# Last attention head: where the eight blocks of the output projection stand among its score blocks

## The chip, the cores and the metric

The kernel runs on one core of a Trainium2 chip. The metric is the device time of one execution in microseconds (us), as the median of several runs. PE is the matrix engine (PEld its weight loads), DVE the vector engine, ACT the scalar engine, POOL the general one; SP issues most of the DMA transfers.

## The reference

A decoder trunk of two layers on 1024 tokens with 1024 features, in float32. The first layer mixes with a short gated convolution, the second with multi-head attention over a shared compressed key and value; each is followed by a gated feed-forward part. The change lies at the end of the attention:

```python
def causal_block_attention(...):          # per head h, query block of 128
    sc = qn_b . k_nope + qr_b . k_pe      # 128 + 64 features
    p = softmax(where(mask, sc * scale, neg))
    return p @ v
...
h = h + attn.reshape(b, s, N_HEADS * V_HEAD_DIM) @ w_o
h = h + swiglu_ffn(rms_norm(h, mla_ffn_norm_g[j]), ...)
```

There are 8 heads of 128 value features. `h` is the residual stream, and the product with `w_o` sums over all heads.

## The kernel before

**Number format.** Every float32 product is made of three matmuls on a high and a low part of each operand (`split`, L108 to L112: ACT casts the high part, DVE or POOL subtracts for the low part). The residual stream lies transposed: `st.h[n]` holds features 128 n to 128 n + 127 for all 1024 tokens.

**A head.** `scores` (L1459) makes one block of 128 queries against the keys up to it: five terms of matmuls into PSUM, then mask, maximum and scaling on DVE, the exponential on ACT (L1476, the last reader of the PSUM tile), the division on DVE. Blocks 0 to 3 fit one bank (`ps1`), blocks 4 to 7 take a wide buffer of two banks (`ps2`). `pv` (L1481) makes the value product of four query blocks at once: transposes on PE (L1491), casts and subtractions into `pt`, three matmuls per key block (L1500 to L1502). A head has two value products: g = 0 (blocks 0 to 3) and g = 1 (blocks 4 to 7). The second one of a head is kept in `pend` and issued within the next head, ahead of its score blocks 4 and 5 (L1590).

**The loop of the heads** (L1574). Four times per head it issues a pair of score blocks, and behind the pair the jobs that `per` (L1586) names. In heads 0 to 6 the jobs prepare the next head. In head 7 they are eight blocks of the output projection, `project_o(O0, 0, (n,))` for n = 0 to 7: block n makes features 128 n to 128 n + 127 of the attention's output from heads 0 to 4, whose values were written to DRAM and read back (`O0`, L1600). Each block loads its weights into a raw buffer (320 KB), splits them (high part on ACT, low part on POOL, L112), loads `st.h[n]` from DRAM on the SP queue (L1549), runs 30 matmuls of 512 columns (L146 to L150) into a wide PSUM buffer, and adds the result to `st.h[n]` on DVE (L1552).

**Behind the loop** (L1601 to L1605). The weights of heads 5, 6 and 7 are loaded (`wo_load`, raw buffers), those of head 5 split (`wo_parts(5)`, two slots), and the second value product of head 7 issued. Then the stage `pl` adds heads 5 to 7 to `st.h` and leads into the feed-forward part; the splits for heads 6 and 7 are its first steps.

**What is scarce.** "act" slots: 30 tiles of 512 KB, for `h`, keys, values, queries, read-back heads and kept weights. Raw buffers: 5, two of which hold read-back parts (`cq_tile`). High and low weight tiles: 4 each; both parts of a block's weights take low ones (`wsplit`), so two blocks have theirs at a time, and `pt` takes the high ones. PSUM in the attention: two wide buffers and four single banks; `pl` has eight single banks of a new pool.

**What sets the order.** The loop of the heads isn't written as a fixed order: the framework's planner orders each engine's queue before the run, by its own estimate of when operands and buffers are ready, with the order of the text as priority. On the chip every queue then runs in that fixed order. The stages before and after (`Steps.run`) are in an order written out by hand, which the planner keeps.

Of the kernel before, what the change touches and what calls it, by code (L numbers as in the profile page):

```python
# [19 lines left out]
KD = D // P  # L20
# [28 lines left out]
def trunk(ctx, tc, aps, out):  # L49
# [7 lines left out]
    def enter(name):  # L57

        if "stack" in phase:
            phase["stack"].close()  # L60
        phase["stack"] = ExitStack()
        phase["pool"] = phase["stack"].enter_context(tc.tile_pool(name=name, bufs=1, reuse_waits="tile"))
# [21 lines left out]
    def hi_tile(name):  # L84
        return slots.tile([P, S], F32R, name=name, tag="whi", bufs=4)
# [4 lines left out]
    def pslot(name, tag, bufs, dt=F32, shape=None):  # L90
        return phase["pool"].tile(shape or [P, S], dt, name=name, tag=tag, bufs=bufs)
# [10 lines left out]
    def ps1(name):  # L102
        return phase["psum"].tile([P, 512], F32, name=name, tag="ps1", bufs=phase["ps"][1])

    def move(dst, src):
        nc.gpsimd.dma_start(dst, src)


    def split(hi, lo, src, gain=None, eng=None):
        if gain is None:  # L110
            nc.scalar.copy(out=hi, in_=src)  # L111
            (eng or nc.vector).tensor_tensor(lo, src, hi.bitcast(F32), ALU.subtract)  # L112
        else:
            nc.scalar.activation(hi, src, AF.Copy, scale=gain)
            nc.vector.scalar_tensor_tensor(lo, src, gain, hi.bitcast(F32), ALU.mult, ALU.subtract)
# [1170 lines left out]
    def cq_tile(i):  # L1286
        return slots.tile([P, S], F32R, name="cq", tag="raw", bufs=5)
# [122 lines left out]
    def make_k(h, w=None, new=lambda: ps2("ps_k")):  # L1410
        wh, wl = w or W_k(h).all()
        ps = new()
        gemm(ps, lambda k: wh[:, k, :], lambda k: wl[:, k, :], kv_p(0), kv_p(1), range(2))
        Kt[h] = parts_of("k", ps)

    def make_v(h, w=None, quarters=None):

        wh, wl = w or W_v(h).all()
        if h not in Vt:
            Vt[h] = Vt[h + 1] = [(slot("vh", F32R), slot("vl", F32R)) for _ in range(2)]  # L1420
        nt = 4 if quarters is None else 2
        for t4 in range(2) if quarters is None else quarters:
            ps = ps2("ps_v") if nt == 4 else ps1("ps_v")
            for tb in range(nt):
                tok = slice((t4 * nt + tb) * P, (t4 * nt + tb + 1) * P)
                o = ps[:, tb * 256:(tb + 1) * 256]
                for k in range(2):
                    xh, xl = kvs[k].p
                    nc.tensor.matmul(o, lhsT=xh[:, tok], rhs=wh[:, k, :], start=k == 0, stop=False)
                    nc.tensor.matmul(o, lhsT=xh[:, tok], rhs=wl[:, k, :], start=False, stop=False)  # L1430
                    nc.tensor.matmul(o, lhsT=xl[:, tok], rhs=wh[:, k, :], start=False, stop=k == 1)
            c = slice(t4 * nt % 4 * 256, (t4 * nt % 4 + nt) * 256)
            split(*[t[:, c] for t in Vt[h][t4 * nt // 4]], ps)

    def make_q(h, w=None, new=lambda: ps2("ps_q")):
        wh, wl = w or W_q(h).all()
        ps = new()
        gemm(ps, lambda k: wh[:, k, :], lambda k: wl[:, k, :], q_p(0), q_p(1), range(3))
        a, b = parts_of("qn", ps)
        Qt.setdefault(h, {}).update(h=a, l=b)  # L1440

    def make_qr(h, w=None, new=lambda: ps2("ps_q"), eng=nc.gpsimd):

        hi, lo = w or W_qr(h).all()
        ps = new()
        gemm(ps, lambda k: hi[:, k, :], lambda k: lo[:, k, :], q_p(0), q_p(1), range(3))
        qr = tmp("qr")
        rope(qr, ps, eng)
        yh, yl = tmp("qrh", dt=F32R), tmp("qrl", dt=F32R)
        split(yh, yl, qr, eng=eng)  # L1450
        for a in range(2):
            t = slot("qrs", F32R)
            for i, y in enumerate((yh, yl)):
                for q in range(2):
                    r = i * 64 + q * 32
                    move(t[r:r + 32], y[q * 64 + a * 32:q * 64 + a * 32 + 32])
            Qt.setdefault(h + a, {})["r"] = t
# [23 lines left out]
    def pv(V, g, ps_, h):  # L1481

        nb = 4 * g + 4
        o = ps1("ps_pv")
        PT = {}

        def turn(kb):
            c = slice(max(kb - 4 * g, 0) * P, 512)
            t = ps1("ps_t")
            for j in range(c.start // P, 4):  # L1490
                nc.tensor.transpose(t[:, j * P:(j + 1) * P], ps_[j][:, kb * P:(kb + 1) * P], ident)  # L1491
            pt = hi_tile("pt")
            PT[kb] = pt[:, :512], pt[:, 512:]
            split(PT[kb][0][:, c], PT[kb][1][:, c], t[:, c])

        def product(kb):
            c = slice(max(kb - 4 * g, 0) * P, 512)
            vh, vl = [t[:, kb % 4 * 256 + h % 2 * P:kb % 4 * 256 + h % 2 * P + P] for t in V[kb // 4]]
            th, tl = [t[:, c] for t in PT[kb]]
            nc.tensor.matmul(o[:, c], lhsT=vh, rhs=th, start=kb == 0, stop=False)  # L1500
            nc.tensor.matmul(o[:, c], lhsT=vh, rhs=tl, start=False, stop=False)
            nc.tensor.matmul(o[:, c], lhsT=vl, rhs=th, start=False, stop=kb == nb - 1)  # L1502

        for kb in range(nb + 2):
            if kb < nb:
                turn(kb)
            if kb >= 2:
                product(kb - 2)
        gs = slice(g * 512, (g + 1) * 512)
        if h in Od:  # L1510
            split(Od[h][0][:, gs], Od[h][1][:, gs], o)
            return
        oh, ol = (pslot("oh", "oh", 1, F32R, [P, 512]), pslot("ol", "ol", 1, F32R, [P, 512]))
        split(oh, ol, o)
        move(od[h, 0, :, gs], oh)
        move(od[h, 1, :, gs], ol)
# [19 lines left out]
    def load_o(k, hi, lo):  # L1536
        move(hi, od[k, 0])
        move(lo, od[k, 1])
        return hi, lo

    def project_o(O, k0, ns, t=None, final=None):

        nk = len(O)
        hi, lo = wsplit("wo", w_o[:, k0:k0 + nk, ns[0] * P:(ns[-1] + 1) * P], [P, nk, len(ns) * P])
        for i, n in enumerate(ns):
            c = slice(i * P, (i + 1) * P)
            if t is None:
                st.h[n] = slot("h")
                nc.sync.dma_start(st.h[n], hd[n])  # L1549
                ps = ps2("ps_wo")  # L1550
                gemm(ps, lambda k: hi[:, k, c], lambda k: lo[:, k, c], lambda k: O[k][0], lambda k: O[k][1], range(nk))
                nc.vector.tensor_tensor(st.h[n], ps, st.h[n], ALU.add)  # L1552
                continue
            ts = slice(t * 512, (t + 1) * 512)
            ps = ps1("ps_wo")
            for k in range(nk):
                three(ps, hi[:, k, c], lo[:, k, c], O[k][0][:, ts], O[k][1][:, ts], k == 0, k == nk - 1)
            nc.vector.tensor_tensor(st.h[n][:, ts], ps, st.h[n][:, ts], ALU.add)
            final(n, t)
# [14 lines left out]
    for h in range(H):  # L1574
        if h >= 6:
            Od[h] = (tmp("oth", dt=F32R), tmp("otl", dt=F32R))
        if h + 1 < H:
            jobs = [lambda h=h: make_k(h + 1), lambda h=h: make_q(h + 1)]
            if h % 2:
                jobs = [lambda: make_qr(h + 1), lambda: make_v(h + 1)] + jobs  # L1580
        else:
            O1 = [load_o(5, r_(), r_())] + [Od[6], Od[7]]
            jobs = [lambda n=n: project_o(O0, 0, (n,)) for n in range(KD)]
        if h == 0:
            jobs = [lambda: make_q(1)]
        per = {1: ((0,), (), (), ()), 2: ((), (0,), (1,), ()), 4: ((0,), (1,), (2,), (3,)), 8: ((0, 1), (2, 3), (4, 5), (6, 7))}[len(jobs)]  # L1586
        p = []
        for i in range(4):
            if i == 2 and pend:
                pv(*pend.pop(0))  # L1590
            p += [scores(Kt[h], Qt[h], 2 * i + d) for d in range(2)]
            if i == 2:
                pv(Vt[h], 0, p[:4], h)
            if i == 3:
                pend.append((Vt[h], 1, p[4:], h))
            for j in per[i]:
                jobs[j]()
        if h == 6:
            r_ = lambda: slot("oth", F32R)
            O0 = [load_o(k, r_(), r_() if k < 3 else cq_tile(4 - k)) for k in range(5)]  # L1600
# [2 lines left out]
    wo_parts(5)  # L1603
    for u in pend:
        pv(*u)  # L1605
    enter("ffn")
    enter_psum(0, 8)

# [127 lines left out]
```

## Time and profile before

| | us |
|---|---|
| median of 3 runs | 2098.05 |
| lowest and highest | 2097.63, 2100.79 |
| the profiled execution | 2095.82 |
| its span in the profile | 2093.7 |

| engine | busy us | share of the span |
|---|---|---|
| PE | 2053.9 | 98% |
| PEld | 1704.7 | 81% |
| DVE | 1463.5 | 70% |
| ACT | 855.7 | 41% |
| POOL | 269.4 | 13% |

The profile is one execution, recorded by the hardware. A row of the timeline is a run of equal instructions: start, length, engine, line, output and inputs, and in brackets the idle time before it and what ended it. Starts count from the begin of the span. A matmul's end is modelled, so starts are the safer measure.

### The profile page before, as it was taken

What the parts mean: (1) busy time and instruction counts of PE and PEld (TensorE: products, weight loads), DVE (VectorE), ACT (ScalarE), POOL (GpSimd) and SP (SyncE); (2) the same over time, 40 slices, a digit from 0 to 9 for tenths busy, and PEclk for the clock granted to TensorE, in tenths of its full rate; (3) what the DMA queues carried; (4) which work ended last, traced back from release to release, by engine and by line L of the source; (5) the groups of instructions that cost most, each with busy time, mean ns of one, the idle gap of its engine ahead of it and who ended that gap; (6) DMA issues with size and microseconds to landing.
All of it is one profiled execution on the core that took longest, in us unless ns stands there. A gap on an engine that the chain in (4) does not pass through costs nothing.

```text
span 2093.7 us, 25560 instructions
## 1 busy us (share of the span) xinstructions
PE 2053.9 (98%) x9542; PEld 1704.7 (81%) x9542; DVE 1463.5 (70%) x2200; ACT 855.7 (41%) x1440; POOL 269.4 (13%) x388
## 2 busy tenths in 40 slices
PE   7999999999999999999999999989999999999998
PEld 6888888888888887787888888867888888888887
DVE  5996666787667668867577777437887666667556
ACT  7533433533333333354245455225433333333455
POOL 1111100121122110000023322101111111100000
PEclk9999999999999999999999999999999999999999
DMA  7355765596766586554232213425487565686553
GB/s 234 81 133 139 238 239 175 112 220 180 190 163 153 141 287 246 206 206 150 72 70 70 66 52 111 163 81 163 125 201 186 154 160 163 151 286 225 186 169 129
DMA packets 274316, 338.97 MB, mean 162 GB/s; under 512 B 18047, under 2 KB 177984, under 8 KB 273872
## 3 DMA queue, kind: packets, MB, share of 16 engines
q1 hardware_dynamic: 240144, 262.71, 38.8%
q0 software_dynamic: 33888, 74.56, 16.6%
q8 instruction: 74, 1.21, 0.2%
q14 instruction: 50, 0.41, 0.1%
q10 hardware_dynamic: 160, 0.07, 0.0%
HBM read 260.22 MB, written 126.35 MB: 185 GB/s over the span
## 4 chain that ended last, share of the span: by engine, by line
PE 88%; DVE 6%; ACT 2%; issue 2%; DMA 1%; DVEq 0%; SPq 0%; ACTq 0%
PE q L154 17%; PE q L155 17%; PE q L153 17%; PE dn L155 5%; PE dn L153 5%; PE dn L154 5%; PE ps_s L1469 4%; PE pl L153 2%; PE pl L155 2%; PE pl L154 2%; DVE wp_lo L112 1%; PE ps_t L1491 1%; PE ps_l L155 1%; PE ps_l L153 1%; PE ps_l L154 1%
## 5 line engine op out<-in xcount | busy, mean ns | idle before, releaser
L153 PE MATMUL q<-xh,w_hi 128*128 128x512 f32 x1568 | 612.4, 391 | 1.1 <-ACT xh L316 1.1
L154 PE MATMUL q<-xl,w_hi 128*128 128x512 f32 x1568 | 610.5, 389 | 2.3 <-DVE xl L317 2.1
L155 PE MATMUL q<-xh,w_lo 128*128 128x512 f32 x1568 | 610.4, 389 | 0.0
L154 PEld LDWEIGHTS q<-xl,w_hi 128*128 128x128 f32 x1568 | 294.4, 188 | 64.6 <-DVE xl L317 2.8
L153 PEld LDWEIGHTS q<-xh,w_hi 128*128 128x128 f32 x1568 | 294.3, 188 | 63.3 <-ACT xh L316 1.5
L155 PEld LDWEIGHTS q<-xh,w_lo 128*128 128x128 f32 x1568 | 294.3, 188 | 61.0
L112 DVE TENSOR_TENSOR w_lo<-wr,w_hi 128x512 fp32r<-128x512 f32 (+1 forms) x272 | 191.9, 705 | 199.3 <-ACT w_hi L111 197.5
L111 ACT CAST w_hi<-wr 128x512 fp32r<-128x512 f32 (+1 forms) x272 | 170.4, 630 | 293.5 <-DVE wr L390 191.2
L155 PE MATMUL dn<-mp_hi,wp_lo 128*128 128x512 f32 (+1 forms) x628 | 243.9, 388 | 2.6 <-DVE wp_lo L112 0.8
L153 PE MATMUL dn<-mp_hi,wp_hi 128*128 128x512 f32 (+1 forms) x628 | 242.9, 387 | 0.0
L154 PE MATMUL dn<-mp_lo,wp_hi 128*128 128x512 f32 (+1 forms) x628 | 242.0, 385 | 0.0
L1072 POOL COPY paced<-pace 128x1 f32<-128x1 f32 x128 | 75.1, 587 | 1020.4 <-ACT pace L1071 1020.4
L112 DVE TENSOR_TENSOR mp_lo<-m,mp_hi 128x1024 fp32r<-128x1024 f32 x84 | 95.2, 1134 | 120.4 <-ACT mp_hi L111 120.4
L111 ACT CAST mp_hi<-m 128x1024 fp32r<-128x1024 f32 x84 | 82.4, 980 | 221.7 <-PE dn L154 211.5
L155 PEld LDWEIGHTS dn<-mp_hi,wp_lo 128*128 128x128 f32 x628 | 117.9, 188 | 32.7 <-DVE wp_lo L112 9.6
L154 PEld LDWEIGHTS dn<-mp_lo,wp_hi 128*128 128x128 f32 x628 | 118.0, 188 | 23.6
L153 PEld LDWEIGHTS dn<-mp_hi,wp_hi 128*128 128x128 f32 x628 | 118.0, 188 | 23.0 <-DVE h L740 0.2
L112 DVE TENSOR_TENSOR wp_lo<-w,wp_hi 128x1024 fp32r<-128x1024 f32 x84 | 94.8, 1128 | 0.0
L111 ACT CAST wp_hi<-w 128x1024 fp32r<-128x1024 f32 x84 | 82.1, 977 | 0.0
L473 ACT ACTIVATE c<-c 128x512 f32<-128x512 f32 x44 | 27.8, 632 | 131.7 <-DVE c L448 131.7
L1476 ACT ACTIVATE p<-ps_s,mx,rq 128x128 f32<-128x128 f32 (+3 forms) x64 | 53.2, 833 | 55.3 <-DVE mx L1473 50.1
L382 DVE TENSOR_TENSOR w_lo<-wr,w_hi 128x1024 fp32r<-128x1024 f32 x56 | 68.2, 1218 | 7.9 <-ACT w_hi L378 7.9
(296 smaller groups left out, 3231.9 us busy)
## 6 DMA issues: line engine op xcount, KB each, us to landing
m<-md_f SPq DMA_DIRECT2D x70, 512.0 KB, 4.9
md_f<-c SPq DMA_DIRECT2D x110, 256.0 KB, 3.7
wr<-in_conv_ffn_w_dram SPq DMA_DIRECT2D x47, 512.0 KB, 6.3
wr<-in_mla_ffn_w_dram SPq DMA_DIRECT2D x47, 512.0 KB, 5.4
w<-mw_f SPq DMA_DIRECT2D x40, 512.0 KB, 3.9
h<-hd SPq DMA_DIRECT2D x32, 512.0 KB, 9.6
wr<-in_conv_w_in_dram SPq DMA_DIRECT2D x31, 512.0 KB, 5.7
mw_f<-in_conv_ffn_w_dram POOLq DMA_DIRECT2D x30, 512.0 KB, 7.7
```

Of the source, the lines that this page charges most:

```text
L111: nc.scalar.copy(out=hi, in_=src)
L112: (eng or nc.vector).tensor_tensor(lo, src, hi.bitcast(F32), ALU.subtract)
L153: nc.tensor.matmul(ps, lhsT=wh, rhs=xh, start=st, stop=False, **more)
L154: nc.tensor.matmul(ps, lhsT=wh, rhs=xl, start=False, stop=False, **more)
L155: nc.tensor.matmul(ps, lhsT=wl, rhs=xh, start=False, stop=en, **more)
L382: nc.vector.tensor_tensor(lo, self.ra, hi.bitcast(F32), ALU.subtract)
L473: nc.scalar.activation(self.C1[:, 512:], self.C1[:, 512:], self.first)
L1072: nc.gpsimd.tensor_copy(b, a)
L1469: nc.tensor.matmul(ps[:, a:b], lhsT=q[:, qs], rhs=k[:, a:b], start=i == 0, stop=i == 4)
L1476: nc.scalar.activation(p[:, :kw], ps[:, :kw], AF.Exp, bias=mx, scale=rq[:, qb:qb + 1], accum_out=rsum)
L1491: nc.tensor.transpose(t[:, j * P:(j + 1) * P], ps_[j][:, kb * P:(kb + 1) * P], ident)
```

## The change

In head 7 one block of the projection stands behind each pair of score blocks instead of two (blocks 0 to 3), and blocks 4 to 7 stand behind the second value product of head 7, after the kept weights have been loaded and head 5's split. Nothing else is altered.

```diff
-        per = {1: ((0,), (), (), ()), 2: ((), (0,), (1,), ()), 4: ((0,), (1,), (2,), (3,)), 8: ((0, 1), (2, 3), (4, 5), (6, 7))}[len(jobs)]
+        per = {1: ((0,), (), (), ()), 2: ((), (0,), (1,), ()), 4: ((0,), (1,), (2,), (3,)), 8: ((0,), (1,), (2,), (3,))}[len(jobs)]
...
     wo_parts(5)
     for u in pend:
         pv(*u)
+    for j in range(4, KD):
+        jobs[j]()
     enter("ffn")
```

In the text the order of head 7 was: score blocks 0, 1, projection 0, 1, scores 2, 3, projection 2, 3, second value product of head 6, scores 4, 5, first value product of head 7, projection 4, 5, scores 6, 7, projection 6, 7, kept weights, second value product of head 7. It becomes: scores 0, 1, projection 0, scores 2, 3, projection 1, second value product of head 6, scores 4, 5, first value product of head 7, projection 2, scores 6, 7, projection 3, kept weights, second value product of head 7, projection 4 to 7.

## Rows read from the trace of the kernel before

**Rows 1.** The page's first block: span, busy time and share of each engine.

```profile
span 2093.7 us, 25560 instructions
PE 2053.9 (98%) x9542; PEld 1704.7 (81%) x9542; DVE 1463.5 (70%) x2200; ACT 855.7 (41%) x1440; POOL 269.4 (13%) x388
```

**Rows 2.** Waits of PE, 1300 to 1412 us: total us, times, longest.

```profile
PE ps_wo L146 <- DVE h L1552: 3.6, 1, 3.6
PE ps_s L1469 <- ACT p L1476: 3.4, 2, 2.6
```

**Rows 3.** Timeline of PE, 1356 to 1406 us.

```profile
1356.67 0.68 PE L146 MATMUL ps_wo<-oth,wo_hi 128*128 128x512 f32 x2
...
1363.67 0.71 PE L146 MATMUL ps_wo<-oth,wo_hi 128*128 128x512 f32 x2
...
1370.61 0.56 PE L1469 MATMUL ps_s<-kh,qnh 128*128 128x512 f32 x2
...
1372.63 0.60 PE L1491 MATMUL ps_t<-ident,p 128*128 128x128 f32 x4
1375.84 0.73 PE L1469 MATMUL ps_s<-kh,qnh 128*128 128x512 f32 x2 [2.61 <-ACT p L1476]
...
1378.24 0.49 PE L1491 MATMUL ps_t<-ident,p 128*128 128x128 f32 x3
1382.32 1.22 PE L146 MATMUL ps_wo<-oth,wo_hi 128*128 128x512 f32 x2 [3.59 <-DVE h L1552]
...
1385.05 0.70 PE L146 MATMUL ps_wo<-oth,wo_hi 128*128 128x512 f32 x2
...
1397.42 0.49 PE L1491 MATMUL ps_t<-ident,p 128*128 128x128 f32 x3
1398.36 0.50 PE L1500 MATMUL ps_pv<-pt,vh 128*128 128x512 f32 x1 [0.46 <-ACT pt L111]
1399.49 0.50 PE L1501 MATMUL ps_pv<-pt,vh 128*128 128x512 f32 x1 [0.63 <-DVE pt L112]
...
1405.54 0.45 PE L153 MATMUL pl<-oth,wo_h 128*128 128x512 f32 x1
```

**Rows 4.** Timeline of DVE, 1379 to 1399 us.

```profile
1379.92 1.22 DVE L112 TENSOR_TENSOR wo_l<-wo_r,wo_h 128x1024 fp32r<-128x1024 f32 x1
1381.05 1.22 DVE L1552 TENSOR_TENSOR h<-ps_wo,h 128x1024 f32<-128x1024 f32 x1
...
1397.62 1.22 DVE L1552 TENSOR_TENSOR h<-ps_wo,h 128x1024 f32<-128x1024 f32 x1 [3.59 <-PE ps_wo L150]
```

**Rows 5.** Timeline of ACT, the exponential of score block 6.

```profile
1374.60 1.10 ACT L1476 ACTIVATE p<-ps_s,mx,rq 128x896 f32<-128x896 f32 x1 [3.47 <-DVE mx L1473]
```

**Rows 6.** Timeline of the SP queue: the loads of the residual tiles.

```profile
1303.43 6.38 SPq L1549 DMA_DIRECT2D h<-hd  x4
...
1354.21 0.34 SPq L1549 DMA_DIRECT2D h<-hd  x1
...
1377.07 1.55 SPq L1549 DMA_DIRECT2D h<-hd  x3
```

**Rows 7.** Windows of 20 us: busy time of each engine, granted clock, DMA share.

```profile
1380.00:1400.00 20.00, 16.59 (x66) 13.19 (x67) 9.27 (x12) 3.91 (x6) 0.00 (x0) 0.91 0.40 129
```

**Rows 8.** The blocks' raw weights: durations min/median/max, landing; waits of the SP queue.

```profile
L111 ACT CAST wo_hi<-wo_raw x8: 727/729/730, 1283.0 to 1370.4; 128x640 fp32r<-128x640 f32 x8
L112 POOL TENSOR_TENSOR wo_lo<-wo_raw,wo_hi x8: 1562/1566/1571, 1283.8 to 1371.2; 128x640 fp32r<-128x640 f32 x8
DMA to landing us min/median/max: 3.0/3.0/3.8
SPq L127 <- POOL wo_lo L112: 42.9, 5, 26.2
```

**Rows 9.** Chain of work: score block 5; timeline of PE: eight transposes of head 7.

```profile
1354.78 1.77 PE ps_s L1469 x10
...
1336.91 1.06 PE L1491 MATMUL ps_t<-ident,p 128*128 128x128 f32 x8
```

## The prediction

> **What bounds the kernel now.** I read the page's first block first: the matrix engine PE is busy for 98% of the span [rows 1], so the time is the sum of PE's work and of the few places where PE stands. Next come PE's waits over the last head, 1300 to 1412 us. The reader is to see that two waits carry most of it: 3.6 us for an addition into the residual stream (`h`, L1552) and 3.4 us in two waits for an exponential (L1476), 2.6 us of it in one [rows 2]. The PE timeline then shows where they lie [rows 3]. Output block 4 begins at 1356.67, block 5 at 1363.67, score block 6 at 1370.61. After four transposes PE waits 2.61 us, score block 7 starts at 1375.84, and after three more transposes PE waits 3.59 us, until block 6 of the projection starts at 1382.32. The last value product (queries 512 to 1023 of head 7) runs from 1397.42 to 1405.54 with waits of 0.46 and 0.63 us inside, and the first matmul of the next stage, `pl`, begins at 1405.54.
>
> Both long waits come from one knot. The attention PSUM pool has two wide buffers, shared by score blocks 4 to 7 and by all output blocks. When score block 7 is due, score block 6 holds one of them and output block 5 the other. Block 6's buffer comes free with its exponential [rows 5], and PE goes on at 1375.84. Block 5's product was done by 1370.61, but its addition runs only at 1381.05 [rows 4], because its `h` tile was not there: of the eight loads of `h`, four were issued by 1309.81, one at 1354.21, and three only from 1377.07 on, after the first matmuls of score block 7 [rows 6]. That is a count of slots. Of 30 "act" slots, 25 are held until the last scores: ten by the read-back heads 0 to 5 (two of their twelve tiles lie in raw buffers), four by `Od`, four by the values, two by the last keys, three by the last queries and two by the rotary keys. Five are left, so `h` 5 to 7 wait for score block 7, which waits for the buffer that block 5, waiting for `h`, holds, or else for block 6's softmax. The only way out is the slow one.
>
> **The change, part by part.** No instruction is added or removed. On PE 30 matmuls per block are moved for blocks 1 to 7, and with each its weight load and its load of `h` (SP queue), the cast of the weights (ACT), their low part (POOL) and the addition (DVE). The order written here is a priority: the planner takes what is ready, lower numbers first.
>
> Blocks 0 and 1 stay before score blocks 4 and 5; blocks 2 and 3, which stood there too, now come behind them. Before score block 7 only blocks 0, 1 and 2 are due, with three `h` tiles, and block 3 behind it takes the fourth; four are loaded by 1309.81 [rows 6]. Block 2's addition then frees its buffer for score block 7 at once, so the 2.61 us wait goes. No output block with a missing `h` stands in the way any more, so the 3.59 us wait goes. Score block 7's end frees seven slots; with the fifth of before that is eight: four for `h` 4 to 7, four for the kept weights of heads 5 and 6. So nothing behind it waits for a slot except head 7's kept weights, which get theirs when the values are done.
>
> After the two waits six matmuls of block 6 take 2.73 us (1382.32 to 1385.05) [rows 3]. A block's 30 take 6.94 us (1363.67 to 1370.61), that is 0.231 each, so six should take 1.39: the loss is 1.34 us. The granted clock of 1380 to 1400 is 0.91 [rows 7]: PE had worked some 3.5 us of the 9.7 before 1382.32, and the matmuls that follow run at the lower level, 1.2 instead of 2.4 GHz. With the waits gone I expect that loss to go too. The Trainium skill ("TensorE: Matmul & The Clock Gate", Part 1) speaks against counting on it: the monitor that sets the clock runs free of the kernel, so the moment of a fall differs between runs. By that, the loss may be missing from the timed runs of before; nothing in one profile decides it, and rival 4 takes it up.
>
> Removed so far: 2.61 + 3.59 + 1.34 = 7.54 us. The waits inside the last value product, 0.46 + 0.63 = 1.09 us, come from the chain transpose, cast, subtract, with an addition of block 7 (1397.62) ahead of it on DVE [rows 4]. In the changed kernel block 4 stands behind it as filler, if its weights are there in time. I take half, 0.55, between 0 and 1.09. Total 8.09.
>
> Three new waits have to be priced; before shows none of them, only their parts.
> - Block 2 takes the buffer of score block 4. The longest softmax chain shown is that of score block 6, 3.21 us from PE's last scores (1372.63) to the release (1375.84). Over it lie score block 5 (1.77 us) and eight transposes (1.06) [rows 9], and value products. 3.21 - 1.77 - 1.06 = 0.4; between 0 and 1.4 if the transposes run earlier. I take 0.3, near the covered end, since the chain of the narrower block 4 is shorter than 3.21.
> - Block 3 takes the buffer of score block 6: 3.21, covered by score block 7 (1375.84 to 1378.24, 2.40) and by transposes like the three at 1378.24 (0.49): 0.3, between 0 and 0.8.
> - `pl` now follows block 7 instead of a value product. If its first banks are those of block 7, it waits for the addition: block 7's product ended at about 1397.42 and its addition at 1398.84, so 1.42 us [rows 3, 4]; if they are others, 0. Before, `pl` followed PE's last product without a wait; I take 0.5.
>
> New waits: 1.1 us. Net: 8.1 - 1.1 = 7.0 us.
>
> The weights of blocks 4 to 7 are costed at nothing, and the cover must be named. The loads of the three kept heads now stand before theirs and hold the three raw buffers left beside the two that carry read-back heads. Block 4's weights can be loaded only when a kept head has been split, which needs score block 7's slots. I put score block 7's end near 1355, the split's end at 1358; load, cast and low part take 3.0 + 0.73 + 1.57 = 5.3 us [rows 8], so they are ready near 1364. Over that lie block 3 (6.9 us) and the value product (8.1), until about 1369. If that cover is gone, each us that the split is later than some 1363 costs one. The next block's weights need 5.3 us, under a block's 6.9. On DVE the two kept low parts (1.2 us each) may again stand before score block 7's scaling, as the one at 1379.92 did, but block 3 hides it.
>
> The profiled execution took 2095.82 us (span 2093.7 and 2.1 around it); less 7.0 it is 2088.8. It lies 2.23 under the median of the runs shown, 2098.05, and with that the forecast is 2091.0.
>
> **The rivals.** (1) The stop comes back beside the softmax: the planner gives score block 7 the buffer of score block 6 again, for instance because DVE makes block 2's addition late. For it: the planner's order already let a kept low part go ahead of a due addition [rows 4]. Against it: block 2's `h` is there and DVE is free by then. Then 2.61 stays, and the gain is 4.4 us (2093.6), or 3.1 if the clock also falls as before (2095.0).
>
> (2) It does not do what it says: the planner pulls the blocks to where they were, since it only takes the text as a priority. For it: in the trace blocks 0 and 1 run long after their place, between transposes of head 6. Against it: two wide buffers force the order of score and output blocks. Gain 0: 2098.
>
> (3) Slower: blocks 4 to 7 are starved of weights, because one raw buffer carries all four and each load waits until the block before has released it. Place: ahead of each of the four blocks; price 5.3 us each, in full 21 us, less the 7.0: 2112. It turns the gain into a loss from 1.8 us per block. For it: the SP queue waited 42.9 us in five waits for a raw buffer before [rows 8]. Against it: the split of a block waits only for the product two blocks back, whose weight tiles it takes, so one raw buffer is refilled in 5.3 us within a product of 6.9, and before, blocks 6 and 7 ran without a gap from 1385.05 to 1397.42.
>
> (4) The clock's fall belongs to this one execution: the timed runs of before don't hold the 1.34 us, so it can't be gained. For it: it is a single fall, seen in one profile. Against it: it comes right behind the longest standstill of the stage. Gain 7.0 - 1.3 = 5.7 us: 2092.4.
>
> **How the numbers follow.** Two results of this kernel are taken as different from 0.2% on, 4.2 us. The forecast has a chance of 0.55, with its own range from 8.6 us of gain (all new waits zero, the 1.09 gained) to 4.3 (2089.4 to 2093.8); rival 4 has 0.10 and lies in that range. Rival 1 has 0.19, rival 2 has 0.06, rival 3 has 0.10. Faster by over 0.2% is below 2093.85: the forecast, rival 4 and a little of rival 1, 0.67. Within 0.2%: the rest of rival 1, rival 2 and the weak end of rival 3, 0.25. Slower 0.08. For the range I take 2087.5 (those 8.6, and 1.9 for the median, whose three runs spread over 3.2 us) to 2098.5, which takes in rivals 1 and 2.
>
> **What would show it.** Right: score block 7 starts without a wait of 2 us after score block 6; no granted clock under 1.00 between the scores and `pl`; seven or eight `h` loads before the last value product; blocks 4 to 7 back to back behind it; `pl` near 1398.5. Wrong: a wait of PE for a low part of `wo` (rival 3), for an exponential before score block 7 (rival 1), or a `pl` that starts later than 1402.

## The result and the profile after

| | before | after |
|---|---|---|
| median of 4 runs each, us | 2097.88 | 2087.89 |
| lowest and highest | 2097.63, 2100.79 | 2087.49, 2090.56 |
| the profiled execution | 2095.82 | 2087.49 |
| its span | 2093.7 | 2085.4 |

The ratio is 0.9945, 95% interval 0.9933 to 0.9957: between 9.0 and 14.1 us faster. The sign and the mechanism were forecast, the size was not: 7.0 us against 10 by the medians and 11.5 by the ratio. The median of the changed kernel, 2087.89, lies just inside the low end of the range, 2087.5; by the ratio, taken of the 2098.05 that the prediction started from, it is 2086.5, just outside.

The page's first block of the changed kernel answers to [rows 1]. PE is busy 1.9 us less than before, most of it matmuls that no longer run at the lower clock; the rest of the 8.3 us of span is waiting.

```profile
span 2085.4 us, 25560 instructions
PE 2052.0 (98%) x9542; PEld 1704.3 (82%) x9542; DVE 1464.1 (70%) x2200; ACT 855.1 (41%) x1440; POOL 270.9 (13%) x388
```

The waits of PE from 1300 to 1412 us in the changed kernel (total, times, longest) answer to [rows 2]. The 3.6 us for an addition into `h` are gone. Of the two waits for an exponential, 3.4 us, the long one ahead of score block 7 is gone; the other, 0.8 us, lies ahead of head 7 and is still there. A new one of 1.4 us stands ahead of an output block.

```profile
PE ps_wo L146 <- ACT p L1476: 1.4, 1, 1.4
PE ps_s L1469 <- ACT p L1476: 0.8, 1, 0.8
PE ps_pv L1501 <- DVE pt L112: 0.6, 1, 0.6
PE ps_wo L146 <- DMA oth<-od: 0.2, 1, 0.2
```

The timeline of PE answers to [rows 3]. Score block 6 starts at 1349.59, and score block 7 at 1352.19 right behind six transposes: no stop. Block 3 stands 1.42 us at 1356.14. Block 4 follows at 1363.64, and the first matmul of `pl` at 1397.31 without a wait. The value product of head 7 lies among blocks 4 and 5.

```profile
1349.59 0.56 PE L1469 MATMUL ps_s<-kh,qnh 128*128 128x512 f32 x2
...
1351.62 0.82 PE L1491 MATMUL ps_t<-ident,p 128*128 128x128 f32 x6
1352.19 0.71 PE L1469 MATMUL ps_s<-kh,qnh 128*128 128x512 f32 x2
...
1356.14 0.73 PE L146 MATMUL ps_wo<-oth,wo_hi 128*128 128x512 f32 x2 [1.42 <-ACT p L1476]
...
1363.64 0.71 PE L146 MATMUL ps_wo<-oth,wo_hi 128*128 128x512 f32 x2
...
1370.22 0.48 PE L1500 MATMUL ps_pv<-pt,vh 128*128 128x512 f32 x1
...
1397.31 0.39 PE L153 MATMUL pl<-oth,wo_h 128*128 128x512 f32 x1
```

The SP queue's loads, against [rows 6]: two `h` loads beside the read-back of the heads instead of four, then five and one, all eight by 1355.32. The weights of block 4 (`wo_raw`) follow at 1354.82.

```profile
1304.79 0.82 SPq L1549 DMA_DIRECT2D h<-hd  x2
...
1337.29 17.44 SPq L1549 DMA_DIRECT2D h<-hd  x5
1354.82 0.38 SPq L127 DMA_DIRECT2D wo_raw<-in_mla_w_o_dram  x1
1355.32 0.47 SPq L1549 DMA_DIRECT2D h<-hd  x1
```

The 20 us window that answers to [rows 7] (length, busy time of PE, PEld, DVE, ACT, POOL, then the granted clock, DMA share, GB/s) has clock 1.00.

```profile
1380.00:1400.00 20.00, 20.00 (x92) 16.64 (x91) 4.37 (x4) 1.32 (x2) 1.58 (x1) 1.00 0.18 52
```

**The sum by starts.** A matmul's end is modelled, so I add up, from the first score matmul of head 7 to the first of `pl`, by how much each start comes later than the columns issued before it need (0.227 us for 512, the usual distance of two starts here at granted clock 1.00). Both kernels issue the same 423 matmuls there: from first to last start 95.79 us before, 86.23 after, 9.57 us less by the unrounded starts. The rows below add up to 11.94 and 2.41; in each kernel another 5.1 us is lost in small steps, most of it behind transposes, and cancels.

| us lost in this stretch | before | after |
|---|---|---|
| ahead of score block 7 | 2.83 | 0 |
| ahead of block 6 | 3.80 | 0 |
| matmuls at 1.2 GHz | 1.37 | 0 |
| inside head 7's last value product | 1.58 | 0 |
| near 1313 to 1318 (start of head 7) | 2.36 | 0.83 |
| ahead of block 3 | 0 | 1.58 |

Behind `pl` the two profiles run alike (688.2 and 688.1 us to the end). Ahead of head 7 the code is the same, but over the 13 profiled executions of this study its first matmul starts anywhere from 1308.8 to 1312.1; that scatter took 1.3 of the 9.6 back in the pair of profiles.

### The profile page after: what moved, and what is told of

The parts are those of the page before. It is cut to its first block, busy times and chain, and to the rows that moved or that the text cites. A ratio compares the mean times of both kernels' runs of the same rounds, so it can differ in the third digit from the quotient of the medians.

```text
span 2085.4 us, 25560 instructions
## 1 busy us (share of the span) xinstructions
PE 2052.0 (98%) x9542; PEld 1704.3 (82%) x9542; DVE 1464.1 (70%) x2200; ACT 855.1 (41%) x1440; POOL 270.9 (13%) x388
```

## The experiments

In all of them "the stage" is that stretch. Kernels of one group shared the runs of the kernel before: its medians there were 2099.23 us (e1 to e4) and 2099.78 (e5 to e8), 15 runs each.

**e1: only the knot undone.** The kernel before, with block 5 moved behind score blocks 6 and 7.

```diff
-        per = {... 8: ((0, 1), (2, 3), (4, 5), (6, 7))}[len(jobs)]
+        per = {... 8: ((0, 1), (2, 3), (4,), (5, 6, 7))}[len(jobs)]
```

> The order of before, with one block moved: block 5 from behind score blocks 4 and 5 to behind score blocks 6 and 7. No block stands behind the last value product. Theory (the knot of slots and wide buffers): with five blocks due before score block 7 the five h tiles suffice, so both long waits (2.8 and 3.8 us counted in starts) and the clock's loss (1.4) go, and one new wait of 1.6 us ahead of block 5 comes: -6.4 us against before, about 2091.5. Rival (filler: the gain comes from the blocks that stand behind the last value product): nothing gained, 2098 give or take 1.

2090.79 us, ratio 0.9960 (0.9948 to 0.9973), stage 88.27. One block out of the way takes both long waits and the clock's fall together. Timeline of PE of this kernel: score block 7 straight behind score block 6's transposes, block 5 with 0.29; the waits in the value product stay, since nothing is left to fill it.

```profile
1366.95 0.60 PE L1491 MATMUL ps_t<-ident,p 128*128 128x128 f32 x4
1367.31 0.70 PE L1469 MATMUL ps_s<-kh,qnh 128*128 128x512 f32 x2
...
1370.16 0.74 PE L146 MATMUL ps_wo<-oth,wo_hi 128*128 128x512 f32 x2 [0.29 <-ACT p L1476]
...
1392.03 0.50 PE L1500 MATMUL ps_pv<-pt,vh 128*128 128x512 f32 x1 [0.46 <-ACT pt L111]
1393.16 0.50 PE L1501 MATMUL ps_pv<-pt,vh 128*128 128x512 f32 x1 [0.63 <-DVE pt L112]
```

**e2: only the last two blocks moved behind the value product.**

```diff
-        per = {... 8: ((0, 1), (2, 3), (4, 5), (6, 7))}[len(jobs)]
+        per = {... 8: ((0, 1), (2, 3), (4, 5), ())}[len(jobs)]
...
     for u in pend:
         pv(*u)
+    for j in range(6, KD):
+        jobs[j]()
```

> The order of before, with blocks 6 and 7 behind the last value product and blocks 4 and 5 left where they were. Theory (the knot): block 5 is still due before score block 7 without its h tile, so score block 7 still waits 2.8 us and block 6 still waits for block 5's addition (3.8) with the clock falling; only the waits inside the value product (1.6) are filled: -1.6 us, about 2096.3. Rival (filler): two of the four blocks do half the work of the change or more: -5 us, about 2093.

2103.65 us, ratio 1.0017 (1.0007 to 1.0026), stage 100.30: slower, and neither theory had that. PE now waits 6.34 us for block 6's weights. Their load leaves only at 1381.56, because the kept heads, now ahead of it in the text, hold the raw buffers until score block 7 has freed the slots for their split (casts at 1379.12 and 1381.68), and it lands only at 1387.8, where the cast has waited for it. That is rival 3's shortage of weights, in one place instead of four. Of this kernel, one after the other, the timelines of PE, of the SP queue and of ACT:

```profile
1377.01 1.22 PE L1469 MATMUL ps_s<-kh,qnh 128*128 128x512 f32 x2 [2.61 <-ACT p L1476]
...
1388.62 1.22 PE L146 MATMUL ps_wo<-oth,wo_hi 128*128 128x512 f32 x2 [6.34 <-ACT wo_hi L111]
```

```profile
1381.56 4.92 SPq L127 DMA_DIRECT2D wo_raw<-in_mla_w_o_dram  x2
```

```profile
1387.85 0.72 ACT L111 CAST wo_hi<-wo_raw 128x640 fp32r<-128x640 f32 x1 [0.32 <-DMA wo_raw<-in_mla_w_o_dram]
```

**e3: the changed kernel with four `h` loads at the start of head 7**, as before.

```diff
-                st.h[n] = slot("h")
-                nc.sync.dma_start(st.h[n], hd[n])
+                for m in range(4) if n == 0 else (n,) if n > 3 else ():
+                    st.h[m] = slot("h")
+                    nc.sync.dma_start(st.h[m], hd[m])
```

> The changed kernel, with the residual tiles of blocks 0 to 3 all loaded at block 0 (four early loads as in before, instead of two). Theory (the read-back of heads 0 to 4 shares the DMA engines with the early h loads, and the planner orders blocks 0 and 1 by it): the waits around head 6's second value product come back, +1.7 us against the changed kernel, about 2089.6. Rival (that stage got shorter because fewer blocks are due there, whatever is loaded): no difference, 2087.9.

2090.29 us, ratio 0.9961 (0.9949 to 0.9974), stage 88.08, 1.85 more than the changed kernel. The waits of before are back ahead of head 6's second value product (PE):

```profile
1316.99 0.49 PE L1500 MATMUL ps_pv<-pt,vh 128*128 128x512 f32 x1 [0.80 <-ACT pt L111]
1317.83 0.50 PE L1501 MATMUL ps_pv<-pt,vh 128*128 128x512 f32 x1 [0.35 <-DVE pt L112]
```

What releases them is a cast and a subtraction of transposed scores, not a DMA. With four loads the planner lets the value product follow its 12 transposes at once; with two it puts eight matmuls of block 0 (L148, L150) between, as these rows of the changed kernel show. So two things changed together, the traffic and the order, and e5 and e6 part them.

```profile
1315.67 1.94 PE L1491 MATMUL ps_t<-ident,p 128*128 128x128 f32 x12
1317.37 0.71 PE L148 MATMUL ps_wo<-oth,wo_hi 128*128 128x512 f32 x2
...
1319.28 0.39 PE L1500 MATMUL ps_pv<-pt,vh 128*128 128x512 f32 x1
```

**e4: the changed kernel with the kept low parts on POOL.**

```diff
-        split(*wo_kept[k], wo_raw[k])
+        split(*wo_kept[k], wo_raw[k], eng=nc.gpsimd)
```

> The changed kernel, with the low parts of the kept weights made on POOL instead of DVE. Theory (a kept low part of 1.2 us stands on DVE ahead of score block 6's scaling and holds back its exponential, and with it the wide buffer of block 3): the wait of 1.6 us ahead of block 3 falls to 0.4 or 0.5: -1.1 us against the changed kernel, about 2086.8. Rival (the softmax chain alone is as long as the wait): no difference, the 1.6 us stay.

2089.84 us, ratio 0.9956 (0.9943 to 0.9968), stage 86.56. Block 3's wait falls from 1.58 to 0.27 us: in the changed kernel a kept low part on DVE stood ahead of score block 6's scaling (`mx`, L1473), for which the exponential waits. DVE of the changed kernel:

```profile
1353.45 1.23 DVE L112 TENSOR_TENSOR wo_l<-wo_r,wo_h 128x1024 fp32r<-128x1024 f32 x1 [0.21 <-PE ps_s L1469]
1354.59 0.21 DVE L1473 TENSOR_SCALAR mx<-mx,nrq 128x1 f32<-128x1 f32 x1
```

But POOL takes 4.77 us for two low parts, block 4's weights come later, and PE waits there instead (PE of e4):

```profile
1363.21 0.74 PE L146 MATMUL ps_wo<-oth,wo_hi 128*128 128x512 f32 x2 [1.19 <-ACT wo_hi L111]
```

**e5: the changed kernel, with the first two `h` tiles loaded twice.** Four loads, but the changed kernel's order.

```diff
-                nc.sync.dma_start(st.h[n], hd[n])
+                for _ in range(2 if n < 2 else 1):
+                    nc.sync.dma_start(st.h[n], hd[n])
```

> The changed kernel, but the h tiles of blocks 0 and 1 are each loaded twice, so that four loads of 512 KB stand in the SP queue beside the read-back of the heads, as before, while PE keeps the changed kernel's order there (8 matmuls of block 0 between the 12 transposes and the first value product of head 6). Question: where did the 1.67 us of waits near 1313 to 1318 go. Theory O (the order): the waits of before are for the casts and subtractions of the transposed scores (0.83 for L111, 0.33 for L112), and block 0's 8 matmuls, 1.8 us, cover them; the extra loads change nothing: waits there 0.4 us as in the changed kernel, first score matmul of head 7 to first pl matmul 86.2 us (to 86.7), time 2087.7 on the scale of the changed kernel's 2087.9. Theory L (the loads): four loads beside the read-back make the heads land later, and PE stands for them wherever it needs them: 1.2 to 1.7 us of waits for oth come back, 87.4 to 87.9 us, time 2089.2 to 2089.6.

2087.89 us, ratio 0.9947 (0.9934 to 0.9959), stage 87.09. The waits for casts and subtractions stay away, so the order covers them. But block 0 itself waits 1.16 us for `oth`, and the stage is 0.86 longer. That the loads do this is not shown: of the seven profiled executions with four early loads only this one and e9 (1.23) have such a wait, the other five (before, e1, e2, e3, e10) have 0.2 in block 0, like the six with two. The timed runs don't tell the 0.9 us.

```profile
1315.49 1.21 PE L146 MATMUL ps_wo<-oth,wo_hi 128*128 128x512 f32 x4 [1.16 <-DMA oth<-od]
1316.54 1.47 PE L1491 MATMUL ps_t<-ident,p 128*128 128x128 f32 x12
1317.97 0.73 PE L148 MATMUL ps_wo<-oth,wo_hi 128*128 128x512 f32 x2
```

**e6: the kernel before without the residual for blocks 2 and 3.** Two loads fewer, the knot untouched.

```diff
-                nc.sync.dma_start(st.h[n], hd[n])
+                if n not in (2, 3):
+                    nc.sync.dma_start(st.h[n], hd[n])
...
-                nc.vector.tensor_tensor(st.h[n], ps, st.h[n], ALU.add)
+                if n in (2, 3):
+                    nc.vector.tensor_copy(st.h[n], ps)
+                else:
+                    nc.vector.tensor_tensor(st.h[n], ps, st.h[n], ALU.add)
```

> The kernel before, but blocks 2 and 3 of the output projection leave out the residual: no load of h for them, a copy in place of the addition. Slots, score blocks and the order of the last four blocks stay; only two h loads are left beside the read-back of the heads, and PE then has block 0's 8 matmuls ahead of the first value product of head 6, as in the changed kernel. Theory (this part of the gain has nothing to do with the knot at blocks 5 to 7): the waits near 1313 to 1318 fall from 2.04 to 0.4 us, the waits of 2.8 and 3.8 us before score block 7 and block 6 and the fall of the clock stay: stage 94.1 us against 95.8, time 1.6 less than before, ratio 0.9992. Rival (the early waits are of one execution or given back at the knot, where PE waits for DMA anyway): the stage stays at 95.5 or more, ratio 1.0000.

2099.41 us, ratio 0.9997 (0.9988 to 1.0006). The early waits fell from 2.36 to 0.84 us as the theory said, yet the stage took 98.80, 3.0 more than the profile of before. Both waits of the knot are there (2.83 and 3.59 in brackets), and behind each the matmuls ran at half speed, 4.4 us of loss against 1.37; `pl` waited another 1.40 for the last low part of head 7. So 1.5 us gained early is hidden by 3.1 more of clock loss and by the wait of `pl`; the timed runs neither show the 1.5 us nor speak against it. That raised the question whether 1.37 is a usual price for the knot at all.

**e9, e10: the kernel before, unchanged, two more executions.**

> The kernel before, unchanged, once more with a profile: is the fall of the granted clock in the knot of one execution, and is it 1.37 us? Theory C (the clock falls in most executions, behind the wait before score block 7 or the one before block 6, and often for longer than in the profile the forecast was made from): granted clock under 1.00 somewhere in 1368 to 1395, matmuls at the lower level for 3 to 10 us, so a loss of 1.5 to 5 us, and the stage from head 7's first score matmul to the first pl matmul 95.8 to 99.5 us; both long waits (2.6 to 3.0 and 3.6 to 3.8 us) there. Rival E (it belonged to that one execution): clock 1.00 throughout the stage, stage 94.4 us.

> The same kernel before, a second execution with a profile. Theory C: as in the first look, a loss to the clock of 1.5 to 5 us, of another size than there, stage 95.8 to 99.5 us. Rival E: clock 1.00, stage 94.4 us.

The windows of 5 us (columns as above; the granted clock is the third number from the right). First the kernel before in the profile of the forecast, then e9, then e10:

```profile
1375.00:1380.00 5.00, 2.89 (x13) 2.19 (x13) 2.38 (x5) 2.78 (x4) 0.00 (x0) 1.00 0.49 157
1380.00:1385.00 5.00, 2.68 (x6) 2.15 (x7) 4.43 (x6) 1.29 (x2) 0.00 (x0) 0.68 0.92 314
1385.00:1390.00 5.00, 5.00 (x23) 4.08 (x22) 0.00 (x0) 0.00 (x0) 0.00 (x0) 0.98 0.33 96
```

```profile
1375.00:1380.00 5.00, 2.39 (x12) 1.83 (x11) 2.23 (x5) 1.70 (x3) 0.00 (x0) 1.00 0.36 106
1380.00:1385.00 5.00, 1.41 (x7) 0.99 (x6) 4.57 (x6) 2.10 (x3) 0.00 (x0) 0.84 0.96 320
1385.00:1390.00 5.00, 5.00 (x14) 3.85 (x13) 1.39 (x3) 0.67 (x2) 0.00 (x0) 0.50 0.71 204
```

```profile
1375.00:1380.00 5.00, 3.25 (x8) 2.58 (x9) 1.23 (x4) 1.47 (x3) 0.00 (x0) 0.66 0.27 101
1380.00:1385.00 5.00, 1.41 (x8) 1.00 (x7) 4.12 (x6) 1.99 (x3) 0.00 (x0) 0.84 0.89 313
1385.00:1390.00 5.00, 5.00 (x12) 3.85 (x13) 1.84 (x3) 1.12 (x2) 0.00 (x0) 0.50 0.68 200
```

The waits are the same to 0.1 us in all three. Behind the second one six matmuls ran at 1.2 GHz in the forecast's profile, 13 in e9 and 12 in e10, where score block 7 had also run slow behind the first wait. By starts the loss is 1.37, 2.76 and 4.14 us, and the stage 95.79, 97.31 and 98.45. Theory C holds: the forecast was made from the cheapest of the three. e9 and e10 took 2101.18 and 2101.63 us.

**e11: the changed kernel once more.**

> The changed kernel, unchanged, a second execution with a profile. Theory C: nothing to fall for, granted clock 1.00 from the scores to pl, stage 86.2 us within 0.3, the one wait of 1.5 to 1.6 us ahead of block 3. Rival E: the clock falls in this stage too in some execution, stage 87 to 90 us.

Stage 86.61, clock 1.00 in every window of 5 us from 1370 to 1395, the wait ahead of block 3 again 1.58: theory C, with the stage 0.1 outside the 0.3 it allowed. This one timed run took 2090.13 us; behind `pl` its clock did fall, which the section on why takes up.

**e7 and e8: can the 1.58 us go too?** Both put block 4 ahead of the kept loads (the cut below). e7 has e4's edit besides; e8 keeps the low parts on DVE, and issues block 3 between score blocks 6 and 7.

```diff
+    jobs[4]()
     for k in (5, 6, 7):
         wo_load(k)
...
-    for j in range(4, KD):
+    for j in range(5, KD):
```

> The changed kernel with two things: the low parts of the kept weights on POOL instead of DVE, and block 4 issued ahead of the three kept loads, so that its weights don't hang on a raw buffer that a kept head holds; blocks 5 to 7 stay behind the value product. Theory: both waits that the changed kernel and the run with POOL alone showed at this place go, the 1.58 us ahead of block 3 (0.3 stays) and the 1.41 ahead of block 4; block 4's weights are loaded near 1340; blocks 5 to 7 still fill the last value product: stage 85.0 us against 86.2, time 2086.4, ratio to before 0.9939. Rival (weights again): the kept heads are now split later, block 5's weights wait for a raw buffer, and 1 to 5 us of PE waiting for wo_hi or wo_lo come ahead of block 5: stage 86 to 90, time 2087.7 to 2092.

> The changed kernel with block 3 issued between score blocks 6 and 7 and block 4 ahead of the kept loads; the kept low parts stay on DVE. Theory: block 3's 6.9 us cover the softmax of score block 6 (3.2 us and a low part of 1.2), and block 4 takes a buffer whose block has long been added, so the 1.58 us wait ahead of block 3 goes and none takes its place: stage 84.7 us, time 2086.2, ratio to before 0.9938. Rival (slots): score block 7 ends some 5.5 us later, with it come the slots for h and the kept weights, so block 5's weights or the low parts come late: 1 to 4 us of waits for wo_lo or wo_hi ahead of block 5 or inside the value product, stage 86 to 89, time 2087.5 to 2090.5.

e7: 2087.10 us, ratio 0.9941 (0.9929 to 0.9954), stage 85.67, the lowest of all, but not to be told from the changed kernel. Block 4's wait is gone. Block 3's fell to 1.03 (0.87 in brackets) instead of 0.3, because a kept cast on ACT now stands ahead of the exponential:

```profile
1352.87 1.05 ACT L111 CAST wo_h<-wo_r 128x1024 fp32r<-128x1024 f32 x1 [3.30 <-PE ps_s L1469]
1353.82 1.09 ACT L1476 ACTIVATE p<-ps_s,mx,rq 128x896 f32<-128x896 f32 x1
```

e8: 2088.72 us, ratio 0.9950 (0.9937 to 0.9962), stage 86.37: its rival was right. Block 3's wait went, score block 7 ended later, and with it came block 5's weights (PE):

```profile
1369.54 0.73 PE L146 MATMUL ps_wo<-oth,wo_hi 128*128 128x512 f32 x2 [1.02 <-ACT wo_hi L111]
```

## Why the gain was larger than predicted

**The knot: right.** That score block 7 and block 6 waited on one missing `h` tile and one pair of wide buffers is shown by e1, which moves only block 5 and loses both waits and the fall of the clock. All eight `h` loads were out by 1355.32, as forecast. The two terms came out at 2.83 and 3.80 by starts against 2.61 and 3.59, since the brackets leave out the end of the matmul before.

**The clock: the step that failed, a term sized from one profile.** The prediction took 1.34 us, the loss in the one profile it had, and set beside it a rival in which that loss was missing from the timed runs. The error lay on the other side. The loss is there in all five profiled executions that stand at the knot (before, e2, e6, e9, e10) and in none of the eight that don't, and in the three of the kernel before it is 1.37, 2.76 and 4.14 us, 2.76 on average. The timed runs agree: the mean granted clock is 0.9962 in the 30 runs of before beside e1 to e8, 0.9953 and 0.9965 in e2 and e6, which keep the knot, and 0.9981 in the 30 runs of the six kernels without it (e1, e3, e4, e5, e7, e8). Within the 30 of before, time follows it (2097.2 us on average in the four runs at 0.998, 2102.4 in the eight at 0.995).

**The distance from profile to median.** The profile of the forecast lay 2.23 us under the median, and the prediction carried this over to the changed kernel whole. It is made in several places, and only a part belongs to the knot. e9 and e10 have spans 5.7 and 5.2 us longer than that profile: 1.5 and 2.7 of it in the stage, 1.9 and 1.0 ahead of head 7, 2.3 and 1.6 behind `pl`. There the clock falls once more, in both kernels and not always: the granted clock of 1410 to 1440 us is 1.00 in four profiles (before, after, e6, e7) and 0.89 or 0.94 in the other nine, and from the first matmul of `pl` to the end it is 688.1 to 688.4 us in the four and 689.5 to 691.4 in the nine. So the mean clock of a timed run is not the knot's alone. From 1420 to 1600 us, PE of the changed kernel and then of e3 (length, busy time, granted clock, DMA share, GB/s):

```profile
1420.00:1600.00 180.00, 178.67 (x788) 1.00 0.67 181
```

```profile
1420.00:1600.00 180.00, 178.68 (x776) 0.98 0.65 178
```

Stage against stage, the three executions of before (95.8, 97.3, 98.5) and the two of the changed kernel (86.2, 86.6) are 9.2 to 12.2 us apart, 10.8 on average; the ratio says 9.0 to 14.1.

The Trainium skill ("TensorE: Matmul & The Clock Gate", Part 1) was read as a warning that the loss might be absent. It states that the monitor that sets the clock runs free of the kernel, and that the moment at which the clock changes therefore varies; it says so of the rise at a kernel's start, and the prediction applied it to a fall. The three executions agree with that (6, 13 and 12 slow matmuls behind the same wait); it speaks for an uncertain size on both sides.

**What the profile held and the prediction left out: 1.53 us at 1313 to 1318.** The waits ahead of head 6's second value product were outside the stretch it looked at, so the sum put them at nothing, the second step that failed. In the kernel before they are these:

```profile
1317.11 0.51 PE L1500 MATMUL ps_pv<-pt,vh 128*128 128x512 f32 x1 [0.83 <-ACT pt L111]
1317.95 0.53 PE L1501 MATMUL ps_pv<-pt,vh 128*128 128x512 f32 x1 [0.33 <-DVE pt L112]
```

They went because only two `h` loads are due there, and the planner then orders block 0's matmuls into the gap (e3, e6). Less traffic beside the read-back is no part of the 1.53: in both profiles of the pair block 0 waits 0.2 us.

**The last value product: 1.58 against 0.55.** The prediction halved 1.09 for want of certainty. Block 4's weights came in time, and blocks 4 and 5 filled it wholly; the price by starts is also larger than the brackets.

**The new waits: 1.58 against 1.1, all in one place.** Block 2 and `pl` were priced at 0.3 and 0.5 and cost nothing. Block 3 was priced at 0.3, with the remark that a kept low part ahead of score block 7's scaling would be hidden by block 3. It stood ahead of score block 6's scaling, which nothing hides; e4 takes it away and the wait with it.

**The weights of block 4: the right time, by luck.** "Ready near 1364": their low part ended at 1363.76 and the block began at 1363.64. But the load left 3.2 us earlier than the 1358 of the prediction, and took 6.5 us to land at 1361.3 instead of 3.0, behind three loads of `h`; the two errors cancel. It left at 1354.82 because the first kept head's cast had found a slot early (1347.89), and its low part, released by score block 7's matmuls, was done at 1354.68 (the DVE row in e4). The cover that was used is block 3 alone: the planner issued block 4 right behind it, ahead of most of the value product. ACT of the changed kernel:

```profile
1361.39 0.73 ACT L111 CAST wo_hi<-wo_raw 128x640 fp32r<-128x640 f32 x1 [3.17 <-DMA wo_raw<-in_mla_w_o_dram]
```

e2, where no block stands between score block 7 and the starved one, shows 6.3 us of waiting; e4 and e8 show 1.2 and 1.0 us from a small delay.

In the pair of profiles the balance of forecast to measured is then 7.0 to 9.57: 0.46 from the brackets (0.03 of it the clock), 1.03 from the value product, 1.53 left out, less 0.48 for the new waits. The clock at its mean, 2.76 instead of 1.37, brings this to 11.0, near the 10 to 11.5 of the timed runs; that it is the whole of the rest there is not shown. One sum of the prediction does not come out: with the bounds that it states the smallest gain is 7.54 less 3.62, 3.9 us, and not 4.3.

Left open: why the same standstill brings a fall of the clock in one execution and not in the next (the first wait, 2.8 to 3.0 us by starts, did so in e2, e6 and e10, not in before and e9), why it falls again behind `pl` in some executions, and the rest of block 3's wait, which no version here lost without paying for it elsewhere.

## What to carry to other kernels

A wait that PE suffers in a knot costs more than its own length, because the matmuls behind it may run at half speed; price it from several executions, since one profile can show the cheapest, and before carrying the distance between profile and median over to another kernel, see in which stages it arises. Where an order is planned from estimates, look for waits wherever the moved work's loads and buffers used to stand, not only where the work stood. And whoever moves a block behind loads that hold a shared buffer must follow that buffer to the step that frees it: the same move gained 10 to 11.5 us with eight blocks respaced and lost 4 with two.

## What the runs showed of the hardware

Mean granted clock and time go together in executions of one and the same kernel (0.998 and 2097.2 us, 0.995 and 2102.4). The clock's return took 6 to 13 matmuls of 512 columns behind the same wait. In nine of 13 executions the clock fell near 1410 to 1440 us, and the way to the end was 1.1 to 3.3 us longer than in the other four. A load of 320 KB took 3.0 to 3.8 us to land in the kernel before, and 6.2 (e2) and 6.5 us (changed kernel) right behind three loads of 512 KB.
